# Hybrid encoder block on one core: attention bias loaded as laid out and added by VectorE, gate weight halves side by side, running maximum sent in halves

## The chip, the core and the metric

The kernel runs on one core of a Trainium2 chip. TensorE (PE) multiplies, VectorE (DVE), ScalarE (ACT) and GpSimd (POOL) do the rest, and DMA queues, issued here from SyncE (SP) and POOL, bring the data. Each engine works through its own list of instructions in order and waits where it needs another engine's result. The metric is the device time of one execution in microseconds; lower is better.

## The reference

One layer of an encoder block on 256 tokens of width 2048, in float32. A modulation computed from a vector `c` gives shift, scale and gate columns. The first half projects the normed and modulated tokens into two groups of heads, mixes them and adds the result; the second half is a gated MLP with a convolution over positions.

```python
mod = jax.nn.silu(c) @ w_ada[l] + b_ada[l]
sh1, sc1, ga1, sh2, sc2, ga2 = jnp.split(mod, N_MOD, axis=-1)
h = modulate(rms_norm(x, g_norm1[l]), sh1, sc1)
qa, ka, va, oa, gates, qb, kb, vb = jnp.split(h @ w_in[l], IN_SPLITS, axis=-1)
...
h_a = mlstm_bidirectional(q_a, k_a, v_a, g_a)                 # 4 heads x 256, 16 gate columns
...
h_b = from_heads(neighborhood_attention(..., rpb[l]))         # 8 heads x 128
mixed = jnp.concatenate([h_a, h_b], axis=-1) @ w_out[l]
x = x + ga1[:, None, :] * mixed
h = modulate(rms_norm(x, g_norm2[l]), sh2, sc2)
x = x + ga2[:, None, :] * conv_glu(h, w_up[l], conv_w[l], conv_b[l], w_down[l])
return rms_norm(x, g_final)
```

In the neighbourhood attention the 256 tokens are a grid of 4 rows of 64 columns; a token looks at all 4 rows and at 16 columns around its own. Its scores are `q k * scale + bias`, where the bias depends on the distance in rows and columns and on the head (`rpb`). In the mLSTM heads the gates give, per token and direction, a running maximum that scales the scores.

## The kernel before

Activations lie transposed, 128 model columns on the partitions by 256 tokens, in 16 k-tiles of x. A large product is computed in a split format: each fp32 operand becomes a rounded high part and a low part, and three matmuls (high x high, low x high, high x low) are summed. For activations these are the tiles `hh` and `hl`; for weights `wh` and `wl`.

The weights come as a stream of 422 pieces of up to 128 x 1024, in a fixed order: 126 of the input projection, 32 of the output projection, 176 of the up-projection, 88 of the down-projection. For each piece SP issues the load into a `wr` tile, ScalarE copies it to `wh` (L356), VectorE subtracts to get `wl` (L364), and TensorE multiplies it (`mm_w`, L391 to L393, with 24 matmuls for a full piece of two k-tiles, and `mm_x`, L398 to L400). There are three buffers of `wh` and of `wl` (`WH_BUFS`), so the copy of a piece waits until TensorE has finished the piece three before it.

The input projection runs over five groups of k-tiles (1, 2, 4, 4, 5), each group over all 14 column chunks. During the last group and the output projection the attention heads are worked in between the weight pieces. The neighbourhood attention of a head (`natten`) loads the head's bias with two transfers from POOL (L710), in which windows of a padded table overlap, so that the columns come out in reverse. TensorE computes scores (L715) and adds the bias by a matmul with a matrix `rev` that puts the columns in order (L717), both in plain fp32, which takes two passes each. VectorE then adds a column mask and finds the maximum (L725), ScalarE takes exponentials and scales (L731, L736), TensorE transposes (L741) and multiplies with the values (L751). The gates of the mLSTM heads are 16 columns of the input projection with their own weight tiles (`gates`, L1023 to L1025), then a chain on small tiles (`mlstm_gates`), among it a scan for the running maximum in `g_mr`, 4 heads on 4 partitions. Each mLSTM head spreads its row of it over 128 partitions with two plain fp32 matmuls against a column of the identity (L854).

The modulation is 192 pieces of 128 x 1024, fetched by POOL into `ar` tiles (four buffers in the late part). All but the first four are reduced on VectorE by an instruction that multiplies with a row of silu(c) and sums (L489); two such reductions give one column of 128. Their order is fixed: scale and shift of the first norm, gate 1, scale and shift of the second norm by k-tile, gate 2. The normed and modulated tile h of a k-tile (`h_chain`) needs its column of scale for the product (L429, VectorE), its shift for the rounding (L432, ScalarE) and then gives its low part (L434, VectorE). The up-projection's pieces go over the first three column chunks by turns for k-tiles 0 to 9, so that its 16th, 17th and 18th piece are the first that need k-tiles 10 and 11, 12 and 13, 14 and 15.

The order of all instructions is fixed when the program is built. A planner (`Sched`) takes steps of all these chains, each with a cost and conditions, and places the one that can start first on its engine; the modulation's reductions have the lowest priority on VectorE in this part, and a function (`pace`) holds them back from coming too early. The engines then run these lists.

Of the kernel before, what the change touches and what calls it, by code (L numbers as in the profile page):

```python
# [7 lines left out]
F32 = mybir.dt.float32  # L8
F32R = mybir.dt.float32r
AF = mybir.ActivationFunctionType  # L10
ALU = mybir.AluOpType
# [127 lines left out]
NCONST = 3 * P + GW  # L139
# [3 lines left out]
def block_kernel(ctx, tc, xT_d, cols_d, bg_d, rpb_d, ada_d, win_d, wg_d, wout_d, wup_d, wdown_d, const_d, out_d):  # L143
# [434 lines left out]
    nmask = ppool.tile([P, GW], F32, name="nmask")  # L578
    rev = ppool.tile([P, P], F32, name="rev")
# [3 lines left out]
    wgh = ppool.tile([P, KT, 16], F32R, name="wgh")  # L583
    wgl = ppool.tile([P, KT, 16], F32R, name="wgl")
# [17 lines left out]
    gatT = ppool.tile([16, S], F32, name="gatT")  # L602
# [72 lines left out]
    def tables():  # L675
# [4 lines left out]
        nc.sync.dma_start(maskw, const_d[:, P : 3 * P].rearrange("p (d c) -> p d c", d=2))  # L680
        nc.sync.dma_start(nmask, const_d[:, 3 * P : 3 * P + GW])
        nc.sync.dma_start(rev, const_d[:, 3 * P + GW : 4 * P + GW])
        nc.sync.dma_start(bgb, bg_d.to_broadcast([P, 16]))
        yield act(S, flag("rstd1"), lambda: here)
        A.copy(wgh, wg)
        t = yield dve(S)
        V.tensor_sub(wgl, wg, wgh.bitcast(F32))
# [78 lines left out]
    def mlstm_gates():  # L766
# [5 lines left out]
        mr = ppool.tile([4, 2, S], F32, name="g_mr")  # L772
# [3 lines left out]
        for t in range(ST):  # L776
            T.transpose(gp[:, t * 16 : (t + 1) * 16], gatT[:, t * P : (t + 1) * P], ident[0:16, 0:16])
# [38 lines left out]
        V.tensor_copy(mr[:, 1, :], gp[0:4, S : 2 * S])  # L816
        b.give(t)
        for j in range(8):
            s = 1 << j
            yield dve(2 * S)  # L820
            to = mr[:, 0, :] if j == 7 else pools["a"].tile([4, S], F32, name="g_mf", tag="m_h", bufs=2)
# [4 lines left out]
            V.tensor_tensor(mr[:, 1, 0 : S - s], mr[:, 1, 0 : S - s], mr[:, 1, s:S], ALU.max)  # L826
# [601 lines left out]
```

## Time and profile before

| | |
|---|---|
| median of 3 runs | 1280.11 us (1278.9 to 1280.26) |
| span of the profiled execution | 1278.2 us |
| TensorE busy | 1253.4 us (98%) |
| VectorE busy | 908.2 us (71%) |
| ScalarE busy | 680.4 us (53%) |
| chain that ended last | TensorE 95%, ScalarE 3%, VectorE 1%, DMA 1% |
| matmuls L391 to L393 of the up-projection | 3 x 1408, 284 ns each, pipelined |

The profiled execution has a span, from its first to its last instruction, of 1278.2 us; the timed runs lie around 1280. Matmuls overlap their neighbours: a row's own duration is longer than the distance to the next one's start, and it is that distance which a matmul costs in a dense stretch. The same holds for steps of VectorE that stand close. Times within the profile are counted from the span's start. The first half ends at about 500 us with the second norm; the up-projection follows to about two thirds of the rest, then the down-projection.

### The profile page before, as it was taken

What the parts mean: (1) busy time and instruction counts of PE and PEld (TensorE: products, weight loads), DVE (VectorE), ACT (ScalarE), POOL (GpSimd) and SP (SyncE); (2) the same over time, 40 slices, a digit from 0 to 9 for tenths busy, and PEclk for the clock granted to TensorE, in tenths of its full rate; (3) what the DMA queues carried; (4) which work ended last, traced back from release to release, by engine and by line L of the source; (5) the groups of instructions that cost most, each with busy time, mean ns of one, the idle gap of its engine ahead of it and who ended that gap; (6) DMA issues with size and microseconds to landing.
All of it is one profiled execution on the core that took longest, in us unless ns stands there. A gap on an engine that the chain in (4) does not pass through costs nothing.

```text
span 1278.2 us, 24381 instructions
## 1 busy us (share of the span) xinstructions
PE 1253.4 (98%) x9822; PEld 1217.2 (95%) x9822; DVE 908.2 (71%) x1382; ACT 680.4 (53%) x1027; POOL 110.6 (9%) x208
## 2 busy tenths in 40 slices
PE   8999999999999998999999999999999999999996
PEld 6889999999989998999999999999999999999995
DVE  5998879889999997997666666666665645454543
ACT  5986667668767444554444444444443534343442
POOL 1111111123112111010000000000000000000000
PEclk8999999999999998999999999999999999999998
DMA  9999889988888996786667666666655555655552
GB/s 322 408 370 352 298 297 374 338 285 292 298 297 277 376 330 244 263 323 235 217 215 228 217 216 215 224 224 220 202 184 183 182 183 184 193 183 186 185 182 91
DMA packets 91313, 322.55 MB, mean 252 GB/s; under 512 B 10560, under 2 KB 11072, under 8 KB 91200
## 3 DMA queue, kind: packets, MB, share of 16 engines
q1 hardware_dynamic: 63360, 220.84, 50.4%
q0 software_dynamic: 27840, 100.15, 23.3%
q8 instruction: 77, 1.26, 0.4%
q14 instruction: 36, 0.29, 0.1%
HBM read 318.85 MB, written 2.10 MB: 251 GB/s over the span
## 4 chain that ended last, share of the span: by engine, by line
PE 95%; ACT 3%; DVE 1%; DMA 1%; issue 0%; DVEq 0%; POOL 0%
PE acc_u L392 13%; PE acc_u L393 13%; PE acc_u L391 13%; PE acc_r L391 9%; PE acc_r L393 9%; PE acc_r L392 9%; PE acc L391 6%; PE acc L392 6%; PE acc L393 6%; PE acc L398 2%; PE acc L399 2%; PE acc L400 2%; ACT wh L356 1%; PE bank L890 1%; DMA n_raw<-in_rpb 1%; PE bank L850 1%
## 5 line engine op out<-in xcount | busy, mean ns | idle before, releaser
L364 DVE TENSOR_TENSOR wl<-wr,wh 128x1024 fp32r<-128x1024 f32 (+1 forms) x391 | 466.4, 1193 | 292.0 <-ACT wh L356 290.3
L356 ACT CAST wh<-wr 128x1024 fp32r<-128x1024 f32 (+1 forms) x391 | 400.4, 1024 | 467.1 <-PE acc_u L392 221.0
L391 PE MATMUL acc_u<-hh,wh 128*128 128x256 f32 x1408 | 399.8, 284 | 3.4 <-ACT hh L432 3.4
L392 PE MATMUL acc_u<-hl,wh 128*128 128x256 f32 x1408 | 399.7, 284 | 0.1
L393 PE MATMUL acc_u<-hh,wl 128*128 128x256 f32 x1408 | 399.5, 284 | 0.0
L391 PEld LDWEIGHTS acc_u<-hh,wh 128*128 128x128 f32 x1408 | 271.5, 193 | 3.9 <-ACT hh L432 3.9
L392 PEld LDWEIGHTS acc_u<-hl,wh 128*128 128x128 f32 x1408 | 271.5, 193 | 0.4 <-DVE hl L434 0.4
L393 PEld LDWEIGHTS acc_u<-hh,wl 128*128 128x128 f32 x1408 | 271.5, 193 | 0.0
L391 PE MATMUL acc<-hh,wh 128*128 128x256 f32 x640 | 186.8, 292 | 4.6 <-ACT hh L432 2.3
L392 PE MATMUL acc<-hl,wh 128*128 128x256 f32 x640 | 182.2, 285 | 0.0
L393 PE MATMUL acc<-hh,wl 128*128 128x256 f32 x640 | 182.0, 284 | 0.0
L391 PE MATMUL acc_r<-aTh,wh 128*128 128x256 f32 x640 | 179.7, 281 | 0.0
L392 PE MATMUL acc_r<-aTl,wh 128*128 128x256 f32 x640 | 178.6, 279 | 0.0
L393 PE MATMUL acc_r<-aTh,wl 128*128 128x256 f32 x640 | 178.6, 279 | 0.0
L462 POOL DMA_DIRECT2D ar<-in_ada x173 | 91.7, 531 | 716.4 <-DVE modp L489 352.5
L391 PEld LDWEIGHTS acc<-hh,wh 128*128 128x128 f32 x640 | 123.5, 193 | 10.0 <-ACT acc L260 3.6
L392 PEld LDWEIGHTS acc<-hl,wh 128*128 128x128 f32 x640 | 123.6, 193 | 1.0 <-DVE are L457 0.2
L393 PEld LDWEIGHTS acc<-hh,wl 128*128 128x128 f32 x640 | 123.6, 193 | 0.0
L393 PEld LDWEIGHTS acc_r<-aTh,wl 128*128 128x128 f32 x640 | 120.2, 188 | 0.0
L391 PEld LDWEIGHTS acc_r<-aTh,wh 128*128 128x128 f32 x640 | 120.1, 188 | 0.1
L392 PEld LDWEIGHTS acc_r<-aTl,wh 128*128 128x128 f32 x640 | 119.8, 187 | 0.1
L489 DVE CUSTOM_DVE_ANT_0 ar<-ar,srow,modp 128x1024 f32<-128x1024 f32 x87 | 111.1, 1277 | 0.6 <-DMA ar<-in_ada 0.3
(202 smaller groups left out, 1572.1 us busy)
## 6 DMA issues: line engine op xcount, KB each, us to landing
wr<-in_wup SPq DMA_DIRECT2D x176, 512.0 KB, 3.6
ar<-in_ada POOLq DMA_DIRECT2D x173, 512.0 KB, 5.6
wr<-in_wdown SPq DMA_DIRECT2D x88, 512.0 KB, 4.1
wr<-in_win SPq DMA_DIRECT2D x73, 512.0 KB, 5.7
wr<-in_wout SPq DMA_DIRECT2D x32, 512.0 KB, 5.8
wre<-in_win SPq DMA_DIRECT2D x25, 512.0 KB, 5.4
are<-in_ada POOLq DMA_DIRECT2D x15, 512.0 KB, 5.8
wr<-in_win SPq DMA_DIRECT2D x22, 256.0 KB, 5.4
```

The costliest lines, as they stand in the source:

```text
L356: A.copy(wh, raw)
L364: V.tensor_sub(wl, raw, wh.bitcast(F32))
L391: T.matmul(acc[:, n, :], w_h, h[0], start=st, stop=False, skip_group_check=True)
L392: T.matmul(acc[:, n, :], w_h, h[1], start=False, stop=False, skip_group_check=True)
L393: T.matmul(acc[:, n, :], w_l, h[0], start=False, stop=last, skip_group_check=True)
L398: T.matmul(acc[:, t, :], h_h, wh[:, k, :], start=first, stop=False, skip_group_check=True)
L399: T.matmul(acc[:, t, :], h_h, wl[:, k, :], start=False, stop=False, skip_group_check=True)
L400: T.matmul(acc[:, t, :], h_l, wh[:, k, :], start=False, stop=last, skip_group_check=True)
L462: q.dma_start(raw, ada_d[a : a + P * PIECE].rearrange("(p n) -> p n", p=P))
L489: V.tensor_tensor_reduce(raw, raw, srow[:, h * PIECE : (h + 1) * PIECE], 1.0, modp[:, part, k : k + 1] if h else cols[:, c : c + 1], ALU.m ...
L850: T.matmul(sp[:, u * S : (u + 1) * S], kT[:, 2 * h + k, u * P : (u + 1) * P], qT[:, 2 * h + k, :], start=k == 0, stop=k == 1)
L890: T.matmul(nu[1][:, : DH_A + 1], at[d][:, j, :], va[:, u, h, :], start=n == 0, stop=n == len(blocks) - 1)
```

## The change

There are three edits. The bias of a head is now laid out on the host in the order in which it is used, with the mask of the columns in it, and loaded with one transfer; ScalarE scales it, and VectorE adds it in the step that found the maximum before, in the mask's place. The matmul with `rev`, `rev` itself and the mask tile are gone. The high and low halves of the gate weights lie side by side (32 columns), so that a k-tile takes two matmuls; the two halves of the result are added behind the transposes. The running maximum is split into a high and a low half, kept in space that other tiles have left, and spread over the partitions for both directions at once by two matmuls of 512 columns in the split format. The planner's costs of these steps are changed with them.

```diff
-    wgh = ppool.tile([P, KT, 16], F32R, name="wgh")
-    wgl = ppool.tile([P, KT, 16], F32R, name="wgl")
+    wgc = ppool.tile([P, KT, 2, 16], F32R, name="wgc")
...
-            for rl in range(2):
-                src = bass.AP(rpb_d.tensor, (h * 15 + 5 - rl) * 127, [[1, GW], [127, 6], [1, GW]])
-                nc.gpsimd.dma_start(raw[rl * GW : (rl + 1) * GW].rearrange("p (a b) -> p a b", b=GW), src)
-            here = sch.dma(t + 0.65, 512) + N_LATE
-            t = yield pe(1.72, lambda: here, flag(("qb", i), ("kb", i)), both.has())
+            nc.gpsimd.dma_start(raw, rpb_d[h])
+            here = sch.dma(t + 0.65, 400) + N_LATE
+            tr = yield act(384, lambda: here)
+            A.activation(raw, raw, AF.Copy, scale=DH_B ** 0.5)
+            yield pe(0.87, flag(("qb", i), ("kb", i)), both.has())
             b, scp = both.take()
             for u in range(ST):
-                T.matmul(scp[:, u * S : (u + 1) * S], qT[:, h, u * P : (u + 1) * P], kT[:, h, :], start=True, stop=False)
-                j = 2 - 2 * u
-                T.matmul(scp[:, u * S : (u + 1) * S], rev, raw[:, j * GW : (j + 4) * GW], start=False, stop=True)
-            nraw.give(t)
-            t = yield dve(780, nsl.has())
+                T.matmul(scp[:, u * S : (u + 1) * S], qT[:, h, u * P : (u + 1) * P], kT[:, h, :], start=True, stop=True)
+            t = yield dve(780, nsl.has(), lambda: tr)
...
-                V.tensor_tensor_reduce(s[:, u, :].rearrange("p (a b) -> p a b", b=GW), scp[:, u * S : (u + 1) * S].rearrange("p (a b) -> p a b", b=GW),
-                                       nmask.unsqueeze(1).to_broadcast([P, 4, GW]), DH_B ** -0.5, -3e38, ALU.add, ALU.max, mx[:, u : u + 1])
+                j = 2 - 2 * u
+                V.tensor_tensor_reduce(s[:, u, :], scp[:, u * S : (u + 1) * S], raw[:, j * GW : (j + 4) * GW],
+                                       DH_B ** -0.5, -3e38, ALU.add, ALU.max, mx[:, u : u + 1])
...
-            V.tensor_add(gat[:, t], gp[:, t * 16 : (t + 1) * 16], bgb)
+            V.tensor_add(gat[:, t], gp[:, t * 32 : t * 32 + 16], bgb)
+            V.tensor_add(gat[:, t], gp[:, t * 32 + 16 : t * 32 + 32], gat[:, t])
...
+        yield act(2 * S)
+        A.copy(sel, ident[0:4, 0:4])
+        for d in range(2):
+            A.copy(mrh[:, d * S : (d + 1) * S], mr[d])
+        yield dve(2 * S)
+        for d in range(2):
+            V.tensor_sub(mrl[:, d * S : (d + 1) * S], mr[d], mrh[:, d * S : (d + 1) * S].bitcast(F32))
...
-            yield pe(0.86)
-            for d in range(2):
-                T.matmul(mb[:, d * S : (d + 1) * S], ident[0:4, h : h + 1].to_broadcast([4, P]), mr[:, d, :], start=True, stop=True)
+            yield pe(0.46)
+            pick = sel[:, h : h + 1].to_broadcast([4, P])
+            T.matmul(mb, pick, mrh, start=True, stop=False)
+            T.matmul(mb, pick, mrl, start=False, stop=True)
...
-        yield pe(0.33 * (k1 - k0), flag("wg", *(("h", 0, k) for k in range(k0, k1))), both.has())
+        yield pe(0.24 * (k1 - k0), flag("wg", *(("h", 0, k) for k in range(k0, k1))), both.has())
...
-            T.matmul(o, wgh[:, k, :], hT[k][0], start=k == k0, stop=False)
-            T.matmul(o, wgl[:, k, :], hT[k][0], start=False, stop=False)
-            T.matmul(o, wgh[:, k, :], hT[k][1], start=False, stop=k == k1 - 1)
+            w = wgc[:, k].rearrange("p a b -> p (a b)")
+            T.matmul(o, w, hT[k][0], start=k == k0, stop=False)
+            T.matmul(o, w, hT[k][1], start=False, stop=k == k1 - 1)
```

Lines behind the change carry other numbers in the changed kernel; L364, L429, L434 and L489, for example, are L363, L428, L433 and L488 there.

Since the planner sets the order, the change moves instructions on all engines. TensorE at the first two heads of the neighbourhood attention, in the kernel before (`acc` belongs to the projections, `bank` is a bank of PSUM; a step without a count stands for two passes in plain fp32):

```order
L715 MATMUL bank<-r_kb,r_qb 128x256
L717 MATMUL bank<-n_raw,rev 128x256
L715 MATMUL bank<-r_kb,r_qb 128x256
L717 MATMUL bank<-n_raw,rev 128x256
L715 MATMUL bank<-r_kb,r_qb 128x256
L717 MATMUL bank<-n_raw,rev 128x256
L715 MATMUL bank<-r_kb,r_qb 128x256
L717 MATMUL bank<-n_raw,rev 128x256
L391 MATMUL acc<-hh,wh 128x256
```

and in the changed kernel:

```order
L391 MATMUL acc<-hl,wh 128x256
L392 MATMUL acc<-hh,wl 128x256
L709 MATMUL bank<-r_kb,r_qb 128x256 x4
L390 MATMUL acc<-hh,wh 128x256
L391 MATMUL acc<-hl,wh 128x256
```

The four matmuls with the bias are gone, and the scores stand 12 projection matmuls later in the stream. TensorE at the first two mLSTM heads, before (L850 are the scores, L854 spreads the maximum):

```order
L400 MATMUL acc<-wh,hl 128x512
L850 MATMUL bank<-r_qa,r_ka 128x256 x4
L854 MATMUL bank<-g_mr,cols 128x256 x2
L850 MATMUL bank<-r_qa,r_ka 128x256 x4
L854 MATMUL bank<-g_mr,cols 128x256 x2
L398 MATMUL acc<-wh,hh 128x512
```

and now (`wgc` and `g_mrl` hold the two halves of the maximum, `g_sel` picks the head):

```order
L399 MATMUL acc<-wh,hl 128x512
L855 MATMUL bank<-r_qa,r_ka 128x256 x4
L859 MATMUL bank<-wgc,g_sel 128x512
L860 MATMUL bank<-g_mrl,g_sel 128x512
L855 MATMUL bank<-r_qa,r_ka 128x256 x4
L859 MATMUL bank<-wgc,g_sel 128x512
L860 MATMUL bank<-g_mrl,g_sel 128x512
L397 MATMUL acc<-wh,hh 128x512
```

The place among the projections is the same; the kind of the matmul is another. VectorE in the up-projection, where h of k-tile 15 of the second norm is made, before (an `ISA` of L489 with its second row is one reduction of the modulation, `h_t` the product and `hl` the last step of h; the `wl` that stands ahead of `hl` is that of the 18th up-projection piece):

```order
L477 SCALAR_TENSOR_TENSOR acol<-modc,cols 128x1
L429 SCALAR_TENSOR_TENSOR h_t<-xT,acol,rstd 128x256
L489 ISA ar,modp<-ar,srow,cols 128x1024
L489 ISA modp 128x1
L364 TENSOR_TENSOR wl<-wr,wh 128x1024
L489 ISA ar,modc<-ar,srow,modp 128x1024
L489 ISA modc 128x1
L364 TENSOR_TENSOR wl<-wr,wh 128x1024
L434 SCALAR_TENSOR_TENSOR hl<-h_t,modc,hh 128x256
L489 ISA ar,modp<-ar,srow,cols 128x1024
L489 ISA modp 128x1
L364 TENSOR_TENSOR wl<-wr,wh 128x1024
```

and now (the first row is the `wl` of the 20th up-projection piece, the `hl` that of k-tile 14; the `hl` of k-tile 15 is the row behind the last):

```order
L363 TENSOR_TENSOR wl<-wr,wh 128x1024
L433 SCALAR_TENSOR_TENSOR hl<-h_t,modc,hh 128x256
L488 ISA ar,modp<-ar,srow,cols 128x1024
L488 ISA modp 128x1
L488 ISA ar,modc<-ar,srow,modp 128x1024
L488 ISA modc 128x1
L476 SCALAR_TENSOR_TENSOR acol<-modc,cols 128x1
L428 SCALAR_TENSOR_TENSOR h_t<-xT,acol,rstd 128x256
L488 ISA ar,modp<-ar,srow,cols 128x1024
L488 ISA modp 128x1
L488 ISA ar,modc<-ar,srow,modp 128x1024
L488 ISA modc 128x1
```

The last two tiles of h moved behind the `wl` of the 20th piece, and no `wl` stands between the reductions that they need. Ahead of the last residual step of the first half stand 146 reductions in the order before and 140 now.

## Rows read from the trace of the kernel before

**Rows 1.** Stretches: length, busy us (instructions) per engine, granted clock, DMA share, GB/s.

```profile
0.00:87.00 87.00, 79.79 (x499) 67.84 (x500) 72.52 (x131) 69.47 (x125) 14.57 (x31) 0.96 0.96 367
87.00:260.00 173.00, 173.00 (x1271) 164.08 (x1271) 148.76 (x209) 115.35 (x172) 26.41 (x50) 1.00 0.92 330
260.00:500.00 240.00, 238.19 (x1708) 224.76 (x1708) 215.90 (x448) 150.91 (x284) 49.56 (x89) 1.00 0.90 311
510.00:1264.00 754.00, 754.00 (x6315) 753.85 (x6315) 455.10 (x571) 338.31 (x435) 20.06 (x38) 1.00 0.64 207
```

**Rows 2.** Chain that ended last: start us, us, what (x passes).

```profile
126.87 0.23 PE acc L398
...
280.62 0.43 PE bank L717 x2
...
315.96 1.05 PE bank L854 x4
```

**Rows 3.** Timeline of PE: start, us, what, [idle before <- what ended it].

```profile
397.32 0.67 PE L717 MATMUL bank<-n_raw,rev 128*128 128x256 f32 x2 [0.48 <-DMA n_raw<-in_rpb]
```

**Rows 4.** Timeline of PE, gates of the last group.

```profile
253.19 0.28 PE L1024 MATMUL bank<-hh,wgl 128*16 128x256 f32 x1
253.31 0.28 PE L1025 MATMUL bank<-hl,wgh 128*16 128x256 f32 x1
```

**Rows 5.** Timeline of ACT, copy of the 20th up-projection piece.

```profile
556.12 1.05 ACT L356 CAST wh<-wr 128x1024 fp32r<-128x1024 f32 x1 [1.83 <-PE acc_u L392]
```

**Rows 6.** Timeline of DVE in the up-projection, around h of k-tiles 14 and 15.

```profile
541.02 0.48 DVE L434 SCALAR_TENSOR_TENSOR hl<-h_t,modc,hh 128x256 fp32r<-128x256 f32 x1
541.41 1.28 DVE L489 CUSTOM_DVE_ANT_0 ar<-ar,srow,cols 128x1024 f32<-128x1024 f32 x1
...
547.01 0.48 DVE L429 SCALAR_TENSOR_TENSOR h_t<-xT,acol,rstd 128x256 f32<-128x256 f32 x1
547.41 1.28 DVE L489 CUSTOM_DVE_ANT_0 ar<-ar,srow,cols 128x1024 f32<-128x1024 f32 x1
...
548.62 1.22 DVE L364 TENSOR_TENSOR wl<-wr,wh 128x1024 fp32r<-128x1024 f32 x1
549.76 1.28 DVE L489 CUSTOM_DVE_ANT_0 ar<-ar,srow,modp 128x1024 f32<-128x1024 f32 x1
...
552.55 0.48 DVE L434 SCALAR_TENSOR_TENSOR hl<-h_t,modc,hh 128x256 fp32r<-128x256 f32 x1
...
557.21 1.23 DVE L364 TENSOR_TENSOR wl<-wr,wh 128x1024 fp32r<-128x1024 f32 x1 [0.45 <-ACT wh L356]
```

**Rows 7.** Timeline, first attention head: score step on DVE, transposes on PE.

```profile
281.95 0.42 DVE L725 CUSTOM_DVE_ANT_1 n_s<-bank,nmask 128x256 f32<-128x256 f32 x1 [1.11 <-PE bank L717]
...
286.35 0.60 PE L741 MATMUL bank<-cols,n_s 128*128 128x128 f32 x4
```

**Rows 8.** Timeline of PE, 18th up-projection piece: first use of hl(14), of hl(15).

```profile
556.12 0.28 PE L392 MATMUL acc_u<-hl,wh 128*128 128x256 f32 x1
...
557.56 0.28 PE L392 MATMUL acc_u<-hl,wh 128*128 128x256 f32 x1
```

**Rows 9.** The modulation's tile between 500 and 560 us: its transfers.

```profile
DMA to landing us min/median/max: 3.6/5.3/7.1
```

**Rows 10.** Stretches around the second norm, columns as in rows 1.

```profile
496.00:500.00 4.00, 2.66 (x20) 2.41 (x20) 0.88 (x2) 1.89 (x4) 0.21 (x1) 1.00 0.97 349
500.00:504.00 4.00, 0.60 (x3) 0.19 (x1) 2.73 (x7) 2.69 (x5) 0.00 (x0) 0.91 0.07 29
504.00:510.00 6.00, 5.89 (x26) 5.59 (x27) 6.00 (x10) 1.00 (x3) 0.00 (x0) 0.50 0.43 121
```

**Rows 11.** Timeline, first pair of mLSTM heads: a `wl` on DVE, its first use on PE.

```profile
342.21 1.22 DVE L364 TENSOR_TENSOR wl<-wr,wh 128x1024 fp32r<-128x1024 f32 x1
...
343.91 0.28 PE L393 MATMUL acc<-hh,wl 128*128 128x256 f32 x1
```

More of the change, by code (lines that the diff above doesn't have):

```diff
@@ L138 @@
 NCOLS = _at + P
-NCONST = 3 * P + GW
 @with_exitstack
@@ L577, in block_kernel @@
     maskw = ppool.tile([P, 2, P], F32, name="maskw")
-    nmask = ppool.tile([P, GW], F32, name="nmask")
-    rev = ppool.tile([P, P], F32, name="rev")
     triU = ppool.tile([P, P], F32, name="triU")
@@ L601, in block_kernel @@
     gat = ppool.tile([P, ST, 16], F32, name="gat")
-    gatT = ppool.tile([16, S], F32, name="gatT")
+    gatT = ppool.tile([32, S], F32, name="gatT")
     sqt = Slots(SQ_BUFS)
@@ L679, in tables @@
         nc.sync.dma_start(wg, wg_d)
-        nc.sync.dma_start(maskw, const_d[:, P : 3 * P].rearrange("p (d c) -> p d c", d=2))
-        nc.sync.dma_start(nmask, const_d[:, 3 * P : 3 * P + GW])
-        nc.sync.dma_start(rev, const_d[:, 3 * P + GW : 4 * P + GW])
+        nc.sync.dma_start(maskw, const_d.rearrange("p (d c) -> p d c", d=2))
         nc.sync.dma_start(bgb, bg_d.to_broadcast([P, 16]))
         yield act(S, flag("rstd1"), lambda: here)
-        A.copy(wgh, wg)
+        A.copy(wgc[:, :, 0, :], wg)
         t = yield dve(S)
-        V.tensor_sub(wgl, wg, wgh.bitcast(F32))
+        V.tensor_sub(wgc[:, :, 1, :], wg, wgc[:, :, 0, :].bitcast(F32))
         flags["wg"] = t
@@ L771, in mlstm_gates @@
         enm = ppool.tile([P, ST, 2, 4], F32, name="g_enm")
-        mr = ppool.tile([4, 2, S], F32, name="g_mr")
+        mr = [ht()[0:4, :] for _ in range(2)]
+        mrh = wgc[0:4].rearrange("p k a b -> p (k a b)")
+        mrl = ppool.tile([4, 2 * S], F32R, name="g_mrl")
+        sel = ppool.tile([4, 4], F32R, name="g_sel")
         gv = gat.rearrange("p t (d w h) -> p t d w h", d=2, w=2)
@@ L776, in mlstm_gates @@
         for t in range(ST):
-            T.transpose(gp[:, t * 16 : (t + 1) * 16], gatT[:, t * P : (t + 1) * P], ident[0:16, 0:16])
+            T.transpose(gp[:, t * 32 : (t + 1) * 32], gatT[:, t * P : (t + 1) * P], ident[0:32, 0:32])
         te = yield dve(200)
@@ L815, in mlstm_gates @@
         t = yield dve(S)
-        V.tensor_copy(mr[:, 1, :], gp[0:4, S : 2 * S])
+        V.tensor_copy(mr[1], gp[0:4, S : 2 * S])
         b.give(t)
@@ L820, in mlstm_gates @@
             yield dve(2 * S)
-            to = mr[:, 0, :] if j == 7 else pools["a"].tile([4, S], F32, name="g_mf", tag="m_h", bufs=2)
+            to = mr[0] if j == 7 else pools["a"].tile([4, S], F32, name="g_mf", tag="m_h", bufs=2)
             V.tensor_copy(to[:, 0:s], fwd[:, 0:s])
@@ L831, in mlstm_gates @@
             for d in range(2):
-                T.transpose(mp[:, t * 8 + d * 4 : t * 8 + d * 4 + 4], mr[:, d, t * P : (t + 1) * P], ident[0:4, 0:4])
+                T.transpose(mp[:, t * 8 + d * 4 : t * 8 + d * 4 + 4], mr[d][:, t * P : (t + 1) * P], ident[0:4, 0:4])
         t = yield dve(16)
@@ L837, in mlstm_gates @@
         A.activation(enm, enm, AF.Exp, scale=-1.0)
-        gst.update(gi=gi, enm=enm, mr=mr)
+        gst.update(gi=gi, enm=enm, mr=(mrh, mrl, sel))
         flags["gates"] = t
@@ L845, in mlstm @@
             yield pe(1.72, flag("gates", ("qa", i), ("ka", i)), both.has(2))
-            gi, enm, mr = gst["gi"], gst["enm"], gst["mr"]
+            gi, enm = gst["gi"], gst["enm"]
+            mrh, mrl, sel = gst["mr"]
             bs, sp = both.take()
@@ L1380, in lay_out @@
     )
-    rpb = np.zeros((NH_B, 15, 127), np.float32)
-    rpb[:, :, 48:79] = inputs["rpb"][0]
+    rpb = np.full((NH_B, 2, GW, 6, GW), -BIG, np.float32)
+    for c in range(GW):
+        c0 = min(max(c - WIN // 2, 0), GW - WIN)
+        for r in range(2):
+            rpb[:, r, c, :, c0 : c0 + WIN] = inputs["rpb"][0][:, 5 - r : 11 - r, c0 - c + WIN - 1 : c0 - c + 2 * WIN - 1]
     s = np.arange(P)
-    const = np.zeros((P, P + NCONST), np.float32)
+    const = np.zeros((P, 2 * P), np.float32)
     for d, off in enumerate((s[:, None] > s[None, :], s[:, None] < s[None, :])):
-        const[:, (1 + d) * P : (2 + d) * P] = np.where(off, BIG, 0.0)
-    cc = np.arange(GW)
-    start = np.clip(cc - WIN // 2, 0, GW - WIN)[:, None]
-    ok = (cc[None, :] >= start) & (cc[None, :] < start + WIN)
-    const[:, 3 * P : 3 * P + GW] = np.tile(np.where(ok, 0.0, -BIG), (2, 1))
-    const[s, 3 * P + GW + (s // GW) * GW + GW - 1 - s % GW] = DH_B ** 0.5
+        const[:, d * P : (d + 1) * P] = np.where(off, BIG, 0.0)
     cat = lambda ps: np.ascontiguousarray(np.concatenate(ps))
@@ L1397, in lay_out @@
         "bg": np.ascontiguousarray(inputs["b_gates"].reshape(1, 16)),
-        "rpb": rpb,
+        "rpb": rpb.reshape(NH_B, P, 6 * GW),
         "ada": cat(ada),
```

5 lines of the change are left out of this document (3 added, 2 removed).

## The prediction, made before the changed kernel had run

> **What bounds the kernel now.** I read the stretches first, then the chain that ended last, then the places that the change touches. The stretches [rows 1] show TensorE busy for 173.00 of 173 us between 87 and 260, for 238.19 of 240 up to 500, and for 754 of 754 after 510; VectorE is busy for 215.90 of the 240 us of the attention stretch and ScalarE for 150.91. The chain [rows 2] is made of matmuls there, one behind the other. So a matmul pass that disappears between 87 and 1264 us shortens the run by what it occupied, as long as VectorE, the next engine, keeps up. Only before 87 us (79.79 busy of 87) and around the second norm at 500 us does TensorE wait. The figures below are in the profiled execution's own time, a span of 1278.2 us. The median of the runs shown is 1280.11, that is 1.9 us more, which I add at the end.
>
> **The change, part by part. What TensorE loses.** (1) The reversing matmul of the bias: 8 heads with 2 each, 0.43 us for one, a pair of passes [rows 2]: 16 x 0.43 = 6.9 us. (2) The wait of one of them for its bias transfer, 0.48 us [rows 3]; the scores no longer need that transfer. (3) Gates: 16 k-tiles with three matmuls become two; one takes 0.12 us [rows 4] and the width of the weight side does not stretch the 256 columns that are streamed. The first three k-tiles lie where TensorE waits anyway, so 13 x 0.12 = 1.5 us. (4) The running maximum: per head four passes, 1.05 us [rows 2], become two matmuls of 512 columns in the split format. The nearest row is such a matmul of the projections, 0.23 us [rows 2], so 0.46 and some 0.1 of switching: 0.5 saved x 4 heads = 2.0 us (1.4 to 2.4). Together **10.9 us** (9.8 to 11.3).
>
> **What is added and hidden.** ScalarE scales each head's bias (384 wide). The nearest row is a copy of 1024 columns at 1.05 us [rows 5], so at most 8.4 us over the stretch where ScalarE is idle for 89 [rows 1]; its place in the queue is ahead of weight copies, which run up to three pieces ahead of TensorE. VectorE's score step keeps its shape, with the bias in the place of the mask. Two gate adds and the two subtractions of the maximum come to it; a subtraction of 1024 columns takes 1.14 us, start to next start [rows 6], so these are under 3 us, in a stretch where it has 24 idle. The copies of the maximum make the gate chain longer by under 3 us, and between its transposes and its other readers stand 12 projection matmuls and a head's scores. One bias transfer per head instead of two leaves POOL's queue shorter. I book nothing for these, and up to 3 us as a bound. One visible loss: before, head 1's four score and bias matmuls and 24 projection matmuls covered head 0's softmax, 4.4 us from its score step to the transposes [rows 7]; now they cover 0.8 us less: 0.4 us, and as much again for similar places.
>
> **What comes back: the modulation's debt.** VectorE also reduces the modulation's columns, 1.21 us each from start to next start [rows 6], with a placing that takes idle time. A shorter attention stretch leaves it fewer of them: in the program's order 146 of these reductions stand ahead of the last residual of the first half before, 140 now. The debt of six, 7.3 us, is nearly the time that TensorE gains. It falls due at the second modulated norm: h for k-tiles 14 and 15 cannot be formed until their scale and shift are reduced, and the 18th up-projection piece multiplies by them.
> Before, VectorE finishes h(14) at 541.42 and h(15) at 552.95, a step of 0.40 from start to next start [rows 6], and TensorE first uses them at 556.12 and 557.56 [rows 8]. The slack of h(15) was 4.6 us. Now the order has h(14) behind the weight subtraction of the 20th piece, and that cannot start early: its copy waits for a buffer which TensorE frees as it ends the 17th piece, so the copy starts at 556.12 [rows 5] and the subtraction at 557.21 [rows 6]. From there, with the durations of these rows: subtraction 1.14, h(14) 0.40, so h(14) at 558.75 against 556.12: a wait of 2.6 us. Behind it stand two reductions, the scale (0.07), the product of h(15) (0.40), two more reductions, and h(15) itself: 4 x 1.21 + 0.87 = 5.7, so 564.5. TensorE, shifted by 2.6, wanted it at 560.2: another 4.3 us. The stall is **6.9 us**. Bounds: 6.0, if VectorE runs a little closer; 8.5, if the last two reductions wait for their columns, whose four buffers refill in 3.6 to 7.1 us [rows 9].
>
> **The clock after the stall.** The granted clock stood at 1.00 while TensorE was idle for a third of 496 to 500, and fell to 0.50, the lower level of 1.2 GHz, after 3.4 idle us of 500 to 504; it stayed there for the 6 us of 504 to 510 [rows 10], in which TensorE was busy and so did 3.0 us less work. The new stall is longer in sum, but it is split by the 1.4 us of k-tile 14's matmuls, and no row shows such a pattern. I take a fall, at the late part of the stall, so that most of the half-rate time is work: 2.6 us (0 to 3.4).
> The Trainium skill, page "TensorE: Matmul & The Clock Gate", section "Why this matters for your kernels", says that idle gaps between bursts of matmuls bring the array back to half rate. The trace agrees at 504 us; for a split gap no run here shows it yet, and without the fall the sum below would be 2.6 us less.
>
> **The sum.** 1278.2 - 10.9 + 0.8 + 6.9 + 2.6 = 1277.6 of span, and 1.9 around it: **1279.5 us**, 0.6 below the median. That is no difference: about 0.2%, 2.6 us, is what a measurement of this kernel can tell from none.
>
> **The rivals.** (A) The clock holds through the split stall. All else as above: 1276.9 us, just on the faster side. For it speaks that matmuls interrupt the gap; against it the fall at the second norm, where matmuls also stood in the idle time.
> (B) The debt costs nothing: the gain stands whole, 1280.1 - 10.9 + 0.8 = 1270.0. It would need VectorE to catch up before the 18th piece; the fixed order speaks against it, as h(14) stands behind a subtraction that TensorE itself releases.
> (C) Slower: VectorE becomes the engine that sets the pace of the attention stretch. The weight subtraction at 342.21 took 1.22 and ended only 0.5 us ahead of the matmul at 343.91 that needs it [rows 11]. If in the first two rounds of heads TensorE arrives earlier and then waits for such subtractions, the four heads' reversing matmuls (3.5 us) and two heads' maximum (1.0) are saved for nothing, and the stall at the 18th piece still comes: 1279.5 + 4.5 = 1284.0. It decides from where the savings between two subtractions pass the slack, 0.5 us at the tightest place; against it, VectorE does six reductions less there.
> (D) The scaled bias arrives late and ScalarE's queue stands behind it: the transfer that TensorE waited for cost 0.48 us once [rows 3]; eight of those are under 4 us and most are covered by the weight buffers. I leave it inside the bounds.
>
> **How the numbers follow.** Forecast case 0.60 (1277.6 to 1282.6), A 0.15, B 0.07, C and its like 0.18. The range takes in A and C and the unknown ends (gain 9.8 to 11.3, stall 6.0 to 8.5, clock 0 to 3.4, up to 3 of the hidden work) but not B: 1275.5 to 1284.5. Faster is A, B and the low edge of the forecast case, 0.23; the same 0.59; slower, C and its like, 0.18.
>
> **What would show it.** In the changed profile: no reversing matmul, two 512-column matmuls per head in the maximum, and TensorE's work up to the second norm shorter by about 10 us, so that the first up-projection matmul starts near 494 instead of 504. Then, some 52 us later, two idle stretches of TensorE of about 2.6 and 4.3 us that end with VectorE's h step, with a granted clock of 0.50 behind them, and six reductions packed around them. If the stall is there and the clock stays at 1.00, A holds; if it is missing, B; if the first up-projection matmul starts near 499 and VectorE's subtractions end the waits between 280 and 360, C. What would make the prediction wrong altogether is an early part, before 87 us, that moves by more than a microsecond or two, since there TensorE waits for copies whose engine the planner has chosen anew.

## The result: a quarter of a per cent slower

The changed kernel takes 1283.09 us (median of 8 runs, 1281.03 to 1284.68) where the kernel before takes 1279.89 in the same session; the ratio is 1.0025 (95% interval 1.0014 to 1.0036). The time lies in the forecast range of 1275.5 to 1284.5 us, but the forecast, 1279.5, said "no difference", and the difference is one that can be measured, with the other sign than the 0.6 us of the forecast. The profiled execution has a span of 1281.6 us.

Stretches of the changed kernel, columns as in [rows 1]. The first four answer to [rows 1], the next two to [rows 10]; the last four are the two places where the time went.

```profile
0.00:87.00 87.00, 80.44 (x496) 68.01 (x497) 71.13 (x128) 69.13 (x125) 14.03 (x30) 0.96 0.95 362
87.00:260.00 173.00, 172.60 (x1266) 164.07 (x1266) 150.66 (x218) 115.96 (x173) 26.94 (x51) 1.00 0.92 333
260.00:500.00 240.00, 233.37 (x1671) 219.68 (x1670) 215.29 (x445) 156.38 (x300) 39.68 (x75) 0.99 0.85 297
510.00:1264.00 754.00, 746.96 (x6238) 745.97 (x6238) 458.92 (x578) 334.93 (x430) 22.69 (x43) 1.00 0.65 209
...
494.00:498.00 4.00, 0.55 (x3) 0.29 (x1) 3.06 (x8) 3.02 (x6) 0.00 (x0) 0.91 0.15 61
498.00:504.00 6.00, 5.93 (x27) 5.64 (x27) 5.76 (x10) 1.00 (x3) 0.00 (x0) 0.50 0.49 137
...
305.00:310.00 5.00, 3.22 (x22) 2.78 (x21) 5.00 (x9) 4.97 (x12) 0.71 (x2) 0.95 0.96 338
310.00:315.00 5.00, 5.00 (x17) 3.88 (x16) 3.03 (x6) 2.45 (x5) 1.39 (x3) 0.71 0.73 219
...
549.00:556.00 7.00, 2.89 (x20) 2.29 (x19) 6.45 (x12) 1.46 (x2) 1.59 (x3) 0.95 1.01 384
556.00:562.00 6.00, 3.06 (x13) 2.83 (x14) 5.29 (x9) 0.51 (x1) 1.58 (x3) 0.50 0.90 293
```

TensorE is no longer busy throughout: it is idle for 1.8 us between 305 and 310, and for 7 of the 13 us from 549 to 562, each time with a lower granted clock behind it. The list of TensorE's waits between 87 and 1264 us (what waited, for what: us in total, times, longest) names both:

```profile
PE acc_u L390 <- ACT hh L431: 9.6, 3, 4.8
PE acc L397 <- ACT acc L259: 1.8, 1, 1.8
...
PE acc_u L391 <- DVE hl L433: 0.9, 1, 0.9
```

Of the 9.6 us, 3.4 belong to the second norm, which the kernel before has too.

Every kernel multiplies the same pieces of weight, so the traces can be laid beside each other piece by piece. The table gives how much later (+) or earlier (-) than in the kernel before a piece begins: the first of the dense stretch (at 87.39 us before), what is won or lost from there to the first up-projection piece (504.05), from there to the end of the last (1264.55), and the sum; then the time at which VectorE finished h(15), and the ratio of the medians with its interval.

| kernel | at 87 us | 87 to 504 | 504 to end | sum | h(15) at | ratio |
|---|---|---|---|---|---|---|
| changed | +0.48 | -6.82 | +9.48 | +3.14 | 559.4 | 1.0025 (1.0014 to 1.0036) |
| bias alone | +1.14 | -3.11 | +6.36 | +4.39 | 560.2 | 1.0033 (1.0020 to 1.0046) |
| gates alone | +2.23 | -1.96 | +0.19 | +0.46 | 556.4 | 0.9987 (0.9978 to 0.9995) |
| maximum alone | +0.83 | -2.02 | +5.51 | +4.32 | 560.2 | 1.0040 (1.0027 to 1.0054) |
| maximum copied by VectorE | +0.77 | -8.10 | +10.10 | +2.77 | 557.9 | 1.0028 (1.0017 to 1.0039) |
| debt off VectorE | +1.07 | +0.02 | -0.05 | +1.04 | 557.1 | 0.9998 (0.9989 to 1.0007) |
| the same, before | +0.03 | +11.09 | +0.13 | +11.25 | 555.3 | 1.0092 (1.0077 to 1.0108) |
| scale on q | +1.25 | -8.13 | +9.69 | +2.81 | 558.0 | 1.0018 (1.0009 to 1.0028) |
| scale on q, debt off | -0.94 | -3.68 | +1.86 | -2.76 | 549.9 | 0.9994 (0.9985 to 1.0004) |
| needed later | +1.28 | -6.82 | +6.72 | +1.18 | 563.6 | 1.0003 (0.9993 to 1.0013) |
| true pace | +0.60 | -7.16 | -0.35 | -6.91 | 529.7 | 0.9956 (0.9941 to 0.9971) |
| the same, before | +3.37 | -0.46 | -0.37 | +2.54 | 539.1 | 1.0015 (1.0006 to 1.0024) |
| true pace, scale on q | +1.48 | -10.24 | -0.13 | -8.89 | 526.9 | 0.9929 (0.9915 to 0.9944) |

The kernel before finished h(15) at 553.0. The first column is from one execution each: "changed" and "needed later" have the same program up to the second norm and differ there by 0.80 us, and the profiled execution of "gates alone" took 1280.43 us where the median of that kernel is 1277.85. So the first column, and the sum with it, is not read to a microsecond. The next column is steadier: it agrees within 0.01 us between "changed" and "needed later".

### The profile page after: what moved, and what is told of

It is laid out like the page before. It is cut to its first block, busy times and chain, and to the rows that moved or that the text cites. A ratio compares the mean times of both kernels' runs of the same rounds, so it can differ in the third digit from the quotient of the medians.

```text
span 1281.6 us, 24268 instructions
## 1 busy us (share of the span) xinstructions
PE 1248.5 (97%) x9766; PEld 1211.8 (95%) x9766; DVE 910.8 (71%) x1386; ACT 682.8 (53%) x1038; POOL 103.9 (8%) x200
## 3 DMA queue, kind: packets, MB, share of 16 engines
q8 instruction: 76, 1.25, 0.4%
## 4 chain that ended last, share of the span: by engine, by line
PE 94%; ACT 3%; DVE 1%; DMA 0%; issue 0%; DVEq 0%; SPq 0%; ACTq 0%
PE acc_u L391 13%; PE acc_u L390 13%; PE acc_u L392 13%; PE acc_r L390 9%; PE acc_r L392 9%; PE acc_r L391 9%; PE acc L390 6%; PE acc L391 6%; PE acc L392 6%; PE acc L397 2%; PE acc L398 2%; PE acc L399 2%; ACT wh L355 1%; PE bank L896 1%; PE bank L855 1%; PE bank L709 1%
## 5 line engine op out<-in xcount | busy, mean ns | idle before, releaser
L363 DVE TENSOR_TENSOR wl<-wr,wh 128x1024 fp32r<-128x1024 f32 (+1 forms) x391 | 466.4, 1194 | 292.3 <-ACT wh L355 290.3
L488 DVE CUSTOM_DVE_ANT_0 ar<-ar,srow,modp 128x1024 f32<-128x1024 f32 x87 | 111.2, 1278 | 0.5
```

The source lines that it names most:

```text
L363: V.tensor_sub(wl, raw, wh.bitcast(F32))
L488: V.tensor_tensor_reduce(raw, raw, srow[:, h * PIECE : (h + 1) * PIECE], 1.0, modp[:, part, k : k + 1] if h else cols[:, c : c + 1], ALU.m ...
```

## Experiments

**Each part alone.** Three kernels take one part of the change into the kernel before. The edits, cut to their core:

```diff
  e1_bias_only
-                T.matmul(scp[:, u * S : (u + 1) * S], rev, raw[:, j * GW : (j + 4) * GW], start=False, stop=True)
...
+            A.activation(raw, raw, AF.Copy, scale=DH_B ** 0.5)
  e2_gates_only
-            T.matmul(o, wgh[:, k, :], hT[k][0], start=k == k0, stop=False)
-            T.matmul(o, wgl[:, k, :], hT[k][0], start=False, stop=False)
...
+            T.matmul(o, w, hT[k][0], start=k == k0, stop=False)
  e3_maximum_only
+            T.matmul(mb, pick, mrh, start=True, stop=False)
+            T.matmul(mb, pick, mrl, start=False, stop=True)
```

> The kernel before with the bias edit alone (laid out per head, scaled by ScalarE, added by VectorE); gates and running maximum as before. Theory 1 (each edit saves on TensorE what its rows say, and two things give it back: a crowd on ScalarE near 305 us and the modulation's debt at the 18th up piece): TensorE saves 7.4 - 0.8 = 6.6 us; in the order 142 reductions stand ahead of the last first-half residual (146 before, 140 in the changed kernel), h(15) behind the 20th weight subtraction; so a stall of 3 to 5 us at the 18th piece, 0 to 3 us more from the clock, and 0 to 2 us near 305 us: 1278 to 1283 us, about 1280. Theory 2 (the saving on TensorE is smaller than its rows say, little comes back): the shift at the end of the first half is under 4 us and no idle stretch near 550 us: 1276 to 1278. Theory 3 (the crowd on ScalarE comes from the scaling of the bias alone): an idle stretch of TensorE near 305 us as in the changed kernel, 1.8 us with a granted clock of 0.50 behind it.

> The kernel before with the gate weights side by side alone (two matmuls per k-tile instead of three). Theory 1: saves 13 x 0.12 = 1.5 us on TensorE; 144 reductions ahead of the last residual, h(15) behind the 19th weight subtraction, so at most 1 us of stall at the 18th piece: 1278.5 to 1280 us. Theory 2 (the early part, where the changed kernel was up to 1.2 us late at 20 to 60 us and 0.5 us late at 87 us, is disturbed by this edit, since its ScalarE copies and VectorE adds are other ones): the first dense piece starts 0.5 us later and the time is 1279 to 1280.5.

> The kernel before with the running maximum in halves alone. Theory 1: saves 4 x 0.5 = 2.0 us on TensorE; 143 reductions ahead of the last residual, h(15) behind the 20th weight subtraction: 3 to 5 us of stall at the 18th piece and 0 to 3 us of clock, so slower than before by itself: 1281 to 1285 us; the two copies and the subtraction of the maximum cause no idle time near 305 us, as ScalarE has no bias to scale there. Theory 2 (no debt follows from so small a saving): 1278 us.

Measured: 1284.42, 1277.85 and 1284.46 us against 1280.22. Two of the three parts make the kernel slower by themselves, and the third, the smallest, faster. Up to 504 us the gates save 1.96 (1.5 counted) and the maximum 2.02 (2.0 counted); in both, the wait of 0.48 us for a bias transfer [rows 3] has gone from TensorE's list of waits, so about 0.5 of each is not the part's own. The bias saves 3.11 of the 6.6 counted; the missing 3.5 are two waits of TensorE for ScalarE near 310 us, and the half clock that follows them (a granted clock of 0.66 over 310 to 315 is 1.7 us of lost work). A stretch with the bias alone, and then TensorE's waits from 285 to 320 us:

```profile
310.00:315.00 5.00, 3.88 (x12) 2.78 (x13) 4.03 (x9) 3.39 (x8) 1.06 (x2) 0.66 0.87 298
```

```profile
PE acc L397 <- ACT acc L259: 1.1, 1, 1.1
PE bank L745 <- ACT n_pT L740: 0.7, 1, 0.7
```

Then the modulation's debt comes due: with 142 and 143 reductions ahead of the last residual, the bias gives back 6.36 and the maximum 5.51 us, though the latter had saved only 2.02. With 144 the gates give back 0.19. The mechanism of theory 1 held for all three, the times of two of them did not: 1284.42 lies above the 1278 to 1283 of the bias and 1277.85 below the 1278.5 to 1280 of the gates. Two reductions late cost next to nothing and three cost 5.5 us, more than what had made them late was worth.

**The stretch at 307 us.** ScalarE is the engine that TensorE waits for there. First its work in the 25 us from 285 to 310 in the kernel before, and its two copies that preload TensorE's accumulator for the piece that multiplies `va0`, first used at 311.31:

```profile
285.00:310.00 25.00, 25.00 (x187) 23.88 (x186) 22.83 (x56) 21.70 (x47) 7.90 (x13) 1.00 0.84 244
```

```profile
303.60 0.59 ACT L260 COPY acc<-r_va 128x512 f32<-128x512 f32 x1
...
305.17 0.59 ACT L260 COPY acc<-r_va 128x512 f32<-128x512 f32 x1
```

The same for the changed kernel, with ScalarE's queue ahead of these copies and the matmul that waits:

```profile
285.00:310.00 25.00, 23.22 (x171) 21.97 (x170) 22.98 (x57) 24.61 (x53) 4.44 (x9) 0.99 0.79 268
```

```profile
302.90 0.53 ACT L705 ACTIVATE n_raw<-n_raw 128x384 f32<-128x384 f32 x1
...
303.79 2.01 ACT L355 CAST wh<-wr 128x1024 fp32r<-128x1024 f32 x2
305.68 0.38 ACT L748 CAST hh<-bank 128x256 fp32r<-128x256 f32 x1
305.95 0.19 ACT L826 CAST g_sel<-cols 4x4 fp32r<-4x4 f32 x1
306.04 0.71 ACT L828 CAST wgc<-h_t 4x256 fp32r<-4x256 f32 x2
306.66 0.57 ACT L259 COPY r_qa<-acc 128x512 f32<-128x512 f32 x1
307.13 0.57 ACT L259 COPY r_ka<-acc 128x512 f32<-128x512 f32 x1
307.61 1.20 ACT L259 COPY acc<-r_va 128x512 f32<-128x512 f32 x2
...
308.86 0.50 PE L397 MATMUL acc<-wh,hh 128*128 128x512 f32 x1 [1.78 <-ACT acc L259]
```

ScalarE is busy for 24.61 of 25 us where it had 3.3 us to spare. The preload, done 5.5 us ahead of its use before, is now done 1.8 us after the matmul could have started. Two edits tell what crowds it. The first moves the three copies of the maximum to VectorE:

```diff
  e4_maximum_copied_by_vector
...
-            A.copy(mrh[:, d * S : (d + 1) * S], mr[d])
+            V.tensor_copy(mrh[:, d * S : (d + 1) * S], mr[d])
...
```

> The changed kernel with the three copies of the running maximum and its selector moved from ScalarE to VectorE. Theory 1 (ScalarE, busy 24.6 of the 25 us from 285 to 310, reaches the copies that preload TensorE's accumulator too late; the 0.9 us of maximum copies stand right ahead of them): the idle stretch of 1.8 us near 307 us shrinks by about 0.9 us or goes, and with it the 3.4 us at a granted clock of 0.50; the stall at the 18th up piece stays: 1279.5 to 1282.2 us. Theory 3 (the scaling of the bias alone makes the crowd): the idle stretch stays within 0.3 us and the time at 1283.

Measured 1283.38 us. The wait stayed at 1.8 us, as theory 3 said and theory 1 did not: the copies of the maximum are not what makes the preload late. What went is the fall of the clock, and with it 1.3 us up to 504. Its stretches, and its wait:

```profile
305.00:310.00 5.00, 3.21 (x20) 2.78 (x19) 4.97 (x11) 4.74 (x10) 0.53 (x1) 1.00 0.88 336
310.00:315.00 5.00, 5.00 (x24) 3.50 (x23) 4.88 (x10) 2.48 (x5) 1.59 (x3) 1.00 0.69 245
```

```profile
PE acc L397 <- ACT acc L259: 1.8, 1, 1.8
```

The second edit takes the scaling of the bias away: q is multiplied by the scale as it is copied out of its accumulator.

```diff
  e7_scale_on_q
-            tr = yield act(384, lambda: here)
-            A.activation(raw, raw, AF.Copy, scale=DH_B ** 0.5)
...
-                                       DH_B ** -0.5, -3e38, ALU.add, ALU.max, mx[:, u : u + 1])
+                                       1.0, -3e38, ALU.add, ALU.max, mx[:, u : u + 1])
...
-                put(o, s)
+                put(o, s, DH_B ** -0.5 if last and n == "qb" else None)
```

> The changed kernel without the eight scaling passes of the bias on ScalarE; q is scaled as it is copied out of its accumulator instead, which costs no pass. Theory 1: the crowd on ScalarE from 285 to 310 us is 3 x 0.5 us lighter, and the idle stretch at 307 us with its half clock (3.5 us) goes or shrinks; but VectorE has the same work up to h(15), so what TensorE wins near 307 us is lost again at the 18th up piece, where h(15) comes at 557 to 560 us as before: 1281 to 1283 us. Rival (the two losses add up, each to be had by itself): 1283.1 - 3.5 = 1279.6 us.

Measured 1282.81 us. ScalarE is busy for 21.62 of the 25 us, the wait for the preload is gone and the clock stays at 1.00. Its stretch, and TensorE's waits from 260 to 320 us:

```profile
285.00:310.00 25.00, 24.23 (x188) 23.26 (x187) 23.22 (x56) 21.62 (x44) 4.78 (x9) 1.00 0.81 255
```

```profile
PE bank L745 <- ACT n_pT L740: 0.8, 1, 0.8
PE bank L735 <- ACT n_s L730: 0.7, 1, 0.7
```

So the scaling makes the crowd. Yet by 504 us each of these two kernels has won only 1.3 us over the changed one: the first keeps the wait of 1.8 us, and the second has the two of its list instead. Behind the second norm both meet the stall of the changed kernel. In all three TensorE waits for 1.43, 0.86 and 4.75 us at k-tiles 14 and 15; the longest in the run with the scale on q:

```profile
557.55 0.58 PE L393 MATMUL acc_u<-hh,wh 128*128 128x256 f32 x1 [4.75 <-ACT hh L434]
```

So h(14) and h(15) come earlier where TensorE does, as they would if weight subtractions that TensorE releases stand ahead of them, and not at a time that VectorE's total work fixes. Theory 1 had the time of this run right and its reason wrong. What the two kernels give back beyond 9.48 us (10.10 and 9.69) goes with the clock: while it was at 0.50, TensorE worked for 3.2 us in the changed kernel and for 5.9 and 5.5 in these. The 0.7 and 1.1 us that are left of the gain from 87 us on are too small for the medians, whose intervals overlap with that of the changed kernel.

**The debt.** The timeline of the changed kernel, VectorE around h(14) and h(15), and TensorE's three matmuls that waited:

```profile
550.94 1.23 DVE L363 TENSOR_TENSOR wl<-wr,wh 128x1024 fp32r<-128x1024 f32 x1 [0.45 <-ACT wh L355]
...
551.37 0.38 PE L390 MATMUL acc_u<-hh,wh 128*128 128x256 f32 x1 [1.43 <-ACT hh L431]
...
552.08 0.48 DVE L433 SCALAR_TENSOR_TENSOR hl<-h_t,modc,hh 128x256 fp32r<-128x256 f32 x1
552.48 1.28 DVE L488 CUSTOM_DVE_ANT_0 ar<-ar,srow,cols 128x1024 f32<-128x1024 f32 x1
...
552.62 0.38 PE L391 MATMUL acc_u<-hl,wh 128*128 128x256 f32 x1 [0.86 <-DVE hl L433]
...
557.05 1.28 DVE L488 CUSTOM_DVE_ANT_0 ar<-ar,srow,modp 128x1024 f32<-128x1024 f32 x1
...
558.92 0.49 DVE L433 SCALAR_TENSOR_TENSOR hl<-h_t,modc,hh 128x256 fp32r<-128x256 f32 x1 [0.58 <-ACT hh L431]
558.94 0.58 PE L390 MATMUL acc_u<-hh,wh 128*128 128x256 f32 x1 [4.75 <-ACT hh L431]
```

Four kernels ask what this stall depends on. Two take 16 of its reductions off VectorE, in the changed kernel and, as a control, in the kernel before; a third does so on top of the scale on q:

```diff
  e5_debt_off_vector, e6_debt_off_vector_before, e8_both (with the edit of e7)
...
+                G.tensor_tensor(raw, raw, srow[:, h * PIECE : (h + 1) * PIECE], ALU.mult)
+                t = yield "ACT", 1.2, ()
+                A.activation(raw, raw, AF.Copy, accum_out=(modc if h else modp)[:, part, k : k + 1])
...
-PACE_B = 0
+PACE_B = 12
```

> The changed kernel; of the modulation's 64 reductions for the second norm, the 16 for the shift of k-tiles 8 to 15 leave VectorE: GpSimd multiplies and ScalarE sums; the cap on how early reductions may run is eased by 12 pieces. Theory 1 (from 280 to 560 us VectorE's total work sets when h(15) is there, 553 to 560 us in all kernels so far, whatever TensorE saves): VectorE has 16 x 1.21 = 19.4 us less to do, h(15) is there before the 18th up piece, the idle stretch and the half clock behind it (9.3 us together in the shift between the traces) go, the stretch near 307 us stays: 1283.1 - 9.3 = 1273.8 us, up to 2 more if GpSimd slows VectorE. Theory 2 (the stall comes from the order alone, h(14) and h(15) behind weight subtractions that TensorE itself releases): also less, as the order puts them behind the 14th and 18th subtraction now; it differs by h(15), which would come at 553 and not earlier. Theory 3 (the stall is not what costs): 1283.

> The same relief of VectorE in the kernel before. Theory 1: there is no stall at the 18th up piece to remove, TensorE is busy throughout: within 1 us of 1280. Rival (the relief is a gain of its own, whatever the change): 1275 us or less.

> Both: q scaled at its copy and 16 reductions off VectorE. Theory 1: both losses gone, the saving on TensorE stands: 1283.1 - 9.3 - 3.5 = 1270.3 us, 1270 to 1273. Rival (a third engine becomes late, ScalarE, which has 16 sums more): 1274 to 1280, with idle stretches of TensorE ended by ScalarE between 360 and 500 us.

Measured: 1280.08, 1292.13 and 1279.69 us. The stall at the 18th piece went (-0.05 from 504 to the end in the first), but the gain of 6.82 up to there went too, and the control lost 11 us. The relief was none. Timeline of VectorE and GpSimd in the first of the three:

```profile
458.68 2.78 POOL L511 TENSOR_TENSOR ar<-ar,srow 128x1024 f32<-128x1024 f32 x1
...
459.12 2.62 DVE L1151 TENSOR_TENSOR sq<-sq 128x256 f32<-128x256 f32 x1
...
461.66 1.21 DVE L363 TENSOR_TENSOR wl<-wr,wh 128x1024 fp32r<-128x1024 f32 x1
...
462.80 0.41 DVE L1151 TENSOR_TENSOR sq<-sq 128x256 f32<-128x256 f32 x1
...
465.09 2.75 POOL L511 TENSOR_TENSOR ar<-ar,srow 128x1024 f32<-128x1024 f32 x1
...
465.51 3.42 DVE L363 TENSOR_TENSOR wl<-wr,wh 128x1024 fp32r<-128x1024 f32 x1
```

An addition that takes 0.41 us takes 2.62 beside GpSimd's product, a subtraction of 1.21 takes 3.42: VectorE stands for 2.2 us, which is more than the 1.21 that it was spared. In this trace 15 of the 16 products lengthen an instruction of VectorE, by 31 us in all against the length that such an instruction has elsewhere (its median); 16 x 1.21 = 19.4 us were spared. So VectorE has 12 us more to do and not 19 less, and TensorE then waits for its weight subtractions, as the list of waits from 87 us on says:

```profile
PE acc_r L392 <- DVE wl L363: 5.1, 6, 2.0
```

The Trainium skill, page "SBUF — State Buffer", section "Who interferes with whom", says that a VectorE instruction with two inputs in SBUF and a GpSimd instruction that reads SBUF exclude each other, the later one standing still; these rows agree. As a test of the debt the three runs are spoiled; as a price of that remedy they are clear.

The fourth leaves the first half as it is, and needs h(14) and h(15) four pieces later:

```diff
  e9_need_later
-PROG_TAIL = 3
+PROG_TAIL = 1
```

> The changed kernel, whose up projection takes k-tiles 14 and 15 at the 22nd instead of the 18th piece (the three first accumulators share 7 instead of 5 rounds of k-tiles, 4 pieces or 11.5 us later); the first half is the same, instruction for instruction. Theory 1 (the stall is a due time: h(14) and h(15) come at 552.6 and 559.4 us, whatever TensorE does): they are wanted at 562 and 564 us, so no stall and no half clock behind the second norm, at most 3 us where three accumulators now end close together: 1283.1 - 9.3 = 1273.8, up to 1277. Theory 2 (VectorE has too much to do altogether, and what is not paid at the 18th piece is paid later): h(15) moves to 564 or beyond, stall as before: 1281 to 1284.

Measured 1280.40 us, between the theories. At k-tiles 14 and 15 one wait of 0.9 us is left of 7.0: h(15) comes at 563.6, and TensorE, which began the 22nd piece at 560.8, stands for it in the middle of that piece. Then the three accumulators close within three pieces, and behind them TensorE waits again, until 574.9 us. The matmul that waited for h(15), and the waits from 540 to 600 us:

```profile
563.60 0.39 PE L391 MATMUL acc_u<-hl,wh 128*128 128x256 f32 x1 [0.87 <-DVE hl L433]
```

```profile
PE acc_u L390 <- ACT aTh L1241: 3.9, 1, 3.9
PE acc_u L391 <- DVE hl L433: 0.9, 1, 0.9
```

and the clock falls behind it:

```profile
573.00:580.00 7.00, 5.11 (x24) 5.14 (x25) 6.64 (x15) 3.36 (x9) 0.06 (x1) 0.54 0.26 90
```

So 6.72 us are given back instead of 9.48. A due date moved is not a debt paid.

**The pace that the order was made for.** In the first half VectorE had idle time in all these kernels (busy for 215.29 of the 240 us from 260 to 500 in the changed one). The planner that fixes the order counts TensorE's step of one k-tile at 1.305 us; the traces show 12 matmuls of 0.12, 1.44. One number was set right:

```diff
  e10_true_pace, e11_true_pace_before, e12_true_pace_scale_on_q (with the edit of e7)
-    PIECE_PE = 1.305
+    PIECE_PE = 1.44
```

> The changed kernel with one number of the planner's model set to what the traces show: 1.44 us (12 matmuls of 0.12) instead of 1.305 for TensorE's step of one k-tile. The order it writes then has 152 of the modulation's reductions ahead of the last first-half residual (140 in the changed kernel, 146 before) and h(14), h(15) behind the 10th and 12th weight subtraction (20th both). Theory 1 (VectorE has idle time in the first half, 22 us from 87 to 260 and 23 us from 260 to 500, which an order written for a faster TensorE leaves empty): both losses go, no idle stretch near 307 or 550 us: 1283.1 - 9.3 - 3.5 = 1270.3 us, 1268 to 1274. Theory 2 (VectorE's total work is the limit, and the idle time is not to be had): the 12 reductions more delay the weight subtractions and TensorE waits for them between 260 and 500 us: 1279 to 1283.

> The same number in the kernel before (152 reductions ahead, h(15) behind the 12th subtraction). Theory 1: TensorE had no wait to lose but 0.5 us of a bias transfer: 1279 to 1281 us, so that the changed kernel is worth 9 to 10 us against this one. Rival (the new order is a gain of its own): 1275 or less.

> Both: the planner's step at 1.44 us, and q scaled at its copy instead of the bias on ScalarE. Theory 1: ScalarE has 8 passes of 0.5 us less, which were hidden once the order is right: within 1.5 us of the run with the true pace alone, 1268 to 1272. Rival (the scaling passes still cost TensorE time): 3 us or more less than that run.

Measured: 1274.03, 1281.48 and 1270.56 us against 1279.69. The first and the third beat the kernel before, by 0.44% and 0.71%; the control does not. Against that control the change is worth 7.5 us, where 9 to 10 had been expected, and 10.9 with the scale on q; from 87 us on the traces give 6.7 and 9.5. The attention stretch of the first and its waits from 87 to 1264 us:

```profile
260.00:500.00 240.00, 233.13 (x1672) 219.05 (x1671) 227.31 (x473) 155.87 (x298) 44.94 (x85) 0.99 0.90 324
```

```profile
PE acc_u L390 <- ACT hh L431: 3.4, 1, 3.4
PE acc_r L392 <- DVE wl L363: 1.5, 1, 1.5
PE bank L1139 <- ACT sq L1124: 1.3, 1, 1.3
```

and the same stretch of the third:

```profile
260.00:500.00 240.00, 235.15 (x1690) 222.04 (x1689) 230.35 (x481) 154.28 (x294) 44.44 (x84) 0.99 0.90 325
```

VectorE does 12 to 15 us more work in the same 240 us, h(15) is there at 529.7 and 526.9, and neither the stretch near 307 us nor the one near 550 is left. What waits remain near 500 us belong to the second norm. This settles what the stall was: not VectorE's total work, as theory 1 of the runs that take the debt off VectorE had it, but an order that put the reductions too late to use VectorE's idle time. The third run is 3.5 us below the first, where at most 1.5 had been expected: with the scaling passes on ScalarE, and the order that comes with them, TensorE still loses some 3 us (7.16 against 10.24 won up to 504 us). A wait of 1.5 us for a weight subtraction and one of 0.4 for ScalarE are seen as idle time; where the other 1.2 go is not shown.

## Why the prediction was wrong, step by step

- **What TensorE loses: right.** 10.9 less 0.8, or 10.1, was counted for the stretch up to the second norm; 10.24 is what the run with the true pace and the scale on q shows, whose list has no wait between 87 us and the second norm. By parts the fit is looser. Without the 0.5 us of the transfer, which the forecast booked to the bias, the gates save about 1.5 for 1.5 and the maximum about 1.5 for 2.0, inside its bounds of 1.4 to 2.4; for the bias it is 3.11 + 3.5 lost near 310 us = 6.6 for 6.6. The 0.8 us for the softmax that is covered less is shown by no row of its own.
- **The debt: right in its cause, and in its sum partly by luck.** Waits of 2.6 and 4.3 us were forecast at k-tiles 14 and 15, 1.43 + 0.86 = 2.3 and 4.75 came: 7.0 for 6.9. The clock stands at 0.50 from 556 to 562; with it 9.48 us are given back, for 6.9 + 2.6 = 9.5. But of the 2.4 us beyond the waits the clock took only some 1.5: TensorE worked for 3.1 of these 6 us and was idle for the rest. Most of the other 0.9 are matmuls that stand alone on either side of a wait (0.38 and 0.58 us in the rows above, where 0.12 from start to start is usual), which the forecast did not count. The sentence of the Trainium skill, page "TensorE: Matmul & The Clock Gate", section "Why this matters for your kernels", on idle gaps between bursts, which the prediction left open for a split gap, agrees with these rows. Rivals A and B fell.
- **"I book nothing for these": the step that failed.** The prediction set ScalarE's scaling against 89 idle us in a stretch of 240 [rows 1]. The scaling lands where ScalarE has 3.3 of 25 us to spare, and TensorE arrives there 6 us earlier (the piece that began at 306.04 begins at 300.05). The wait is 1.8 us, and the half clock behind it cost 1.3, since that much more is won up to 504 us by the kernel that has the same wait and keeps its clock (maximum copied by VectorE). That is 3.1 of the 10.1 - 6.82 = 3.3 that are missing from the shift. A bound of 3 us was kept for the hidden work, but it did not enter the likeliest case, and 3.3 is more than the bound.
- **Rival C named the place and the sign, and the wrong engine.** TensorE did arrive early and wait in the attention stretch, but for ScalarE's preload of an accumulator, not for VectorE's subtractions. Rival D, the late scaled bias, spoke of the transfer and not of the passes queued behind the scaling.
- **The early part** moved by 0.48 us, which is within the 0.80 by which two executions of one program differ there; it is not shown to come from the change.
- **The sum with the measured terms:** 1277.6 + 3.3 + 0.5 = 1281.4, for a span of 1281.6; the median lies 1.5 above the span, for 1.9.

Left open: which of the other copies in ScalarE's queue would have to move for the preload to be in time, and why the first 87 us are 3.37 us longer in the control with the true pace.

## What to carry to other kernels

Where an order is fixed by a planner, a saving on the bounding engine moves the work of all the others relative to it: count what has to be done on them by which date, and check the planner's speed of the bounding engine against the trace first, since here that one number turned a loss of 0.25% into a gain of 0.44% (0.71% with the scaling passes gone as well). Cover for added work is to be read in the 25 us where it lands and not from the mean over a stage. An engine that is 8% busy is no free place for work if its operands hold up the engine that was to be relieved.

## What the runs showed of the hardware

- GpSimd's product of two SBUF operands (128x1024, 2.4 to 2.8 us, once 3.2) stops a two-input instruction that VectorE starts beside it until the product ends: 0.41 us became 2.62, 1.21 became 3.42. Four residual steps inside such products in the same trace, which read one of their operands from TensorE's accumulator, took 0.47 to 0.49 us, as they do elsewhere.
- Idle stretches of TensorE of the same length, at the same place of almost the same program, did and did not bring the lower clock: after 1.8 us the granted clock is 0.71 over 310 to 315 in the changed kernel, and 1.00 with the maximum copied by VectorE; after waits of 0.7 and 1.1 us, with four matmuls between them, it is 0.66 with the bias alone. The same wait of 1.8 us so cost 1.8 or 3.1 us.
